# One encoder layer on one core: exponentials kept in PSUM, experts in shifted order with two sums

## Chip, cores, metric

One core of a Trainium2 chip runs the whole layer in one launch. The metric is the device time of one execution, in microseconds (us). TensorE (PE) multiplies, VectorE (DVE), ScalarE (ACT) and GpSimd (POOL) work elementwise, SyncE (SP) issues most transfers. PEld is TensorE's weight load.

## What is computed

```python
# x: (1, 2048, 1024) float32
proj = h @ W_in                       # pool 512 | q latent 256 | kv latent 128 | rope key 32
y_pool = pool_mixer(u_pool)           # windowed means less the channel, linear map per group
s = einsum('bqhd,bkhd->bhqk', q, k) * 96**-0.5     # 8 heads, 64 + 32 channels
y_mla = einsum('bhqk,bkhd->bqhd', softmax(s), v)   # bidirectional, v has 64 channels
h = LN(alpha*h + concat(y_pool, y_mla) @ W_out)
# 64 experts, each token goes to 8 of them with normalised weights
f = sum over its experts e of w_e * (silu(h @ Wg[e]) * (h @ Wu[e])) @ Wd[e]   # 1024 -> 256 -> 1024
f += shared expert of the same shape
out = LN(alpha*h + f)
```

## The kernel before

All products are float32 split in a high part (`fp32r`, what TensorE multiplies in one pass) and a low part (the rest): a product is then high x high + high x low + low x high (`mm3`, `split`).

The stages follow one another: projections and pooling (`project`), attention (`attend`), output projection with the first norm and the routing (`mix_and_route`), the experts with the last norm (`experts`). The attention's main loop and the routed experts' loop run under `manual_schedule`: each engine executes its instructions in the order in which the code issues them. GpSimd's queue also holds the indirect transfers, SP's all plain ones; an instruction that waits holds up everything behind it on its engine.

**Attention.** 8 heads x 4 blocks of 512 queries are 32 blocks; a block takes 8 steps `(n, c)` of 256 keys, each in two halves of 128 keys. A step is issued in this order: `scores` of both halves into one `ps2` tile of two PSUM banks (three products a half); two maxima for a later block, each a product `max_mm` into `psx` and a reduction `max_red`; `exps`, two ACTIVATEs over 1024 columns, one exact (`p`) and one rounded (`ph`), both into SBUF; `low` of the step before, which takes `p - ph` into float16 (`pl`, in steps 2 and 5 half of it on GpSimd) and adds `p` to the row sums on GpSimd; `values` of the step before that, two products of `ph` with 128 columns of values (high and low parts side by side) and two of `pl` with 64 columns of float16 values, one into either half of the same accumulator. Once a block come `max_neg`, `evac` (the two halves of the accumulator are added), `sums` (a product with ones, a reciprocal) and `turn` (transposes; `finish` scales the output). `split_out` splits w_out for the next stage in 16 of the blocks.

**Experts.** `jobs` are three of the shared expert (256 tokens each), 64 routed ones by falling number of tokens, then five more of the shared expert. A routed job has `CAPS[r]` slots: 12 jobs of 376 to 304 and 24 of 296 to 264 slots have three tiles of rows (the third narrow), 28 jobs of 256 have two. In `step(j)`: `load_weights(j+1)` issues three transfers of 1 MB into the three `wst` buffers; `load(j+2)` reads the expert's list of tokens (`idx`) and gathers their rows on GpSimd into the five `xg` buffers; `gate_up(j, 0)`; splits of the next weights; `act`; `columns` (transposes of the next job's rows through `psx`); `gate_up(j, 1)`; more splits; then for each tile `down` and `scatter`, an indirect transfer that adds the tile's rows to `acc` in DRAM. A tile of at most 64 rows goes through `down_narrow`. The rows to be scattered stand in three buffers used in turn (`y_tile`). Two transfers that add to the same tensor are issued one after the other's landing.

**The end.** After the last routed job, `fetch` loads `acc` for all tokens in units of 256; the shared expert's last four jobs add into those units (`add`), the job `late` is added by GpSimd (`first_y`), and `finish(b)` normalises each unit in pieces between the products (`pace`).

Of the kernel before, what the change touches and what calls it, by code (L numbers as in the profile page):

```python
# [52 lines left out]
class Layer:  # L53
    def __init__(self, ctx, tc, io):
# [4 lines left out]
        self.psum = ctx.enter_context(tc.tile_pool(name="psum", bufs=1, space=PSUM))  # L59
        d = self.dram  # L60
        # high and low parts of the heads' operands, channels by tokens
# [8 lines left out]
        self.hx = d.tile([S + 128, HX], FT, name="hx")  # L70
        self.acc = d.tile([S + 128, D], FT, name="acc")
        self.table = d.tile([E * S, 1], I32, name="table")
# [3 lines left out]
    def ps2(self):  # L76
        return self.psum.tile([128, 2, 512], FT, name="ps2", bufs=2)

    def psx(self):
        return self.psum.tile([128, 512], FT, name="psx", bufs=2)  # L80
# [18 lines left out]
    # ------------------------------------------------------------------ projections and pooling  # L99
    def project(self, attention):  # L100
        tc, nc, io = self.tc, self.nc, self.io
        with ExitStack() as ctx, ExitStack() as top:
# [75 lines left out]
            def latents(b):  # L178
                """Tokens on partitions; both norms and the rope of the keys."""
# [32 lines left out]
                # latent channels on partitions  # L212
# [15 lines left out]
            def pool_in(b, g2):  # L228
                """Pooling channels on partitions."""
# [25 lines left out]
            def values(b):  # L255
                qk = QK[b]
                for j in range(4):
# [4 lines left out]
                    # the high part fits float16  # L262
                    v16 = xp.tile([128, H, 64], HF, name="v16", bufs=2)
                    src = ps.rearrange("p (h e) -> p h e", h=H)
                    nc.scalar.activation(v16, src, AF.Copy)
                    nc.scalar.activation(v[:, :, 0:64], v16, AF.Copy)
                    nc.vector.tensor_tensor(v[:, :, 64:128], src, v16, op=OP.subtract)
# [3 lines left out]
            def queries(b):  # L271
# [87 lines left out]
            def weave(main, *sides):  # L359
                """The steps of main with those of the others between them, each from a step on."""  # L360
# [6 lines left out]
            for b in range(NB):  # L367
# [26 lines left out]
                else:  # L394
                    # the attention begins as early as it can
# [37 lines left out]
    def split_out(self, k, half):  # L433
        c = slice(half * 512, (half + 1) * 512)
        self.split(self.woh[k][:, c], self.wol[k][:, c], self.wos[k][:, c])

    def attend(self):
        tc, nc, io = self.tc, self.nc, self.io
        with ExitStack() as ctx:
# [3 lines left out]
            V, V16, Q, NM = {}, {}, {}, {}  # L443
# [22 lines left out]
            def load_values(h):  # L466
                V[h] = kp.tile([128, NT, 128], FR, name="v", bufs=2)
                nc.sync.dma_start(V[h].bitcast(FT), self.vs[:, h].rearrange("(t p) e -> p t e", p=128))
                V16[h] = kp.tile([128, NT, 64], HF, name="v16", bufs=2)

            def cast_values(h):
                nc.scalar.activation(V16[h], V[h][:, :, 0:64].bitcast(FT), AF.Copy)
# [22 lines left out]

            def max_red(h, b, i):
                qt, kb = divmod(i, 4)
                if (h, b) not in NM:
                    NM[h, b] = kp0.tile([128, 4, 4], FT, name="m4", bufs=2)
                nc.vector.reduce_max(NM[h, b][:, qt, kb:kb + 1], MP.pop((h, b, i)), axis=AX.X)  # L500

            # one over the sums of a block's queries, and the maxima of the block after next, queries on partitions
# [25 lines left out]
            def turn(n):  # L528
                """Both as rows: the first on 64 partitions, the maxima on the one that takes them in."""
                rn = rows(n)  # L530
                pt = self.psa()
# [3 lines left out]
                if n >= 0:  # L535
                    finish(n, pt)
                if n + 2 < NBLK:
                    max_row(n + 2, pt[96:97])

            ST, PT, ACC, AV = {}, {}, {}, {}  # L540

            def scores(n, c, half):
                h, b = blocks[n]
                k, q = key_columns(h, (2 * c + half) * 128, 128), Q[h, b]
                if half == 0:
                    ST[n, c] = self.ps2()
                st = ST[n, c]
                nc.tensor.matmul(st[:, half], k[:, 0], q[0:97, 0], start=True, stop=False)
                nc.tensor.matmul(st[:, half], k[0:96, 0], q[0:96, 1], start=False, stop=False)
                nc.tensor.matmul(st[:, half], k[0:96, 1], q[0:96, 0], start=False, stop=True)  # L550

            def exps(n, c):
                st = ST.pop((n, c))
# [1024 lines left out]
```

## Time and profile before

| what | us |
|---|---|
| median of 3 runs | 3168.24 |
| lowest, highest | 3163.23, 3185.31 |
| profiled execution, first to last instruction | 3228.7 |

The profile is of one execution of its own; it gives the span and no other time. Its page says for the whole span that TensorE is busy 90%, VectorE 68%, ScalarE 51%, GpSimd 48%; these are averages over stages with different limits. A busy TensorE is not TensorE at its peak, since its products overlap and their ends are modelled: their starts tell the pace.

### The profile page before, as it was taken

How to read it: one execution, taken by the hardware profiler on the slowest of the kernel's cores; microseconds unless marked ns; L12 is line 12 of the kernel's file. 1: busy time of each engine (PE TensorE's matmuls, PEld its weight loads, DVE VectorE, ACT ScalarE, POOL GpSimd, SP SyncE). 2: the span in 40 equal slices, each digit the busy share in tenths (PEclk: the TensorE clock that was granted, in tenths of full speed). 3: DMA queues.
4: the chain of work that ended last, by engine and by line, in shares of the span. 5: the costliest groups of instructions: out<-in, count | busy, mean ns of one | idle time of the engine just before them, and what ended most of it. 6: DMA issues, size and time to landing. Idle time of an engine off the chain costs nothing. (4 is left out here: it accounts for less than half of the span.)

```text
span 3228.7 us, 44106 instructions
## 1 busy us (share of the span) xinstructions
PE 2896.9 (90%) x16127; PEld 2334.6 (72%) x16127; DVE 2185.6 (68%) x3570; ACT 1661.3 (51%) x2531; POOL 1548.9 (48%) x919
## 2 busy tenths in 40 slices
PE   8998999989989999866799999998998899899986
PEld 6886655555555557645699988787777888888886
DVE  5557999999999996646445555455555555555548
ACT  4444666566656662211255655455555565555554
POOL 2123888788788870455223444444443322223223
PEclk9998999999999999878899999999999999999998
DMA  6555012022111015422578887777777788888873
GB/s 192 211 190 185 19 46 53 28 52 52 47 36 43 20 37 189 144 101 70 177 203 235 251 228 212 208 219 209 221 220 214 222 273 258 249 260 265 275 223 124
DMA packets 175595, 521.43 MB, mean 161 GB/s; under 512 B 37392, under 2 KB 68944, under 8 KB 150032
## 3 DMA queue, kind: packets, MB, share of 16 engines
q1 hardware_dynamic: 130160, 368.44, 33.3%
q0 software_dynamic: 45216, 150.13, 19.6%
q8 instruction: 129, 2.11, 0.3%
q14 instruction: 90, 0.74, 0.1%
HBM read 375.93 MB, written 142.57 MB: 161 GB/s over the span
## 5 line engine op out<-in xcount | busy, mean ns | idle before, releaser
L1510 POOL DMA_INDIRECT acc<-big,idx x164 | 280.3, 1709 | 897.9 <-DMA acc<-big,idx 276.1
L87 DVE TENSOR_TENSOR wl<-wst,wh 128x1024 fp32r<-128x1024 f32 x392 | 470.2, 1225 | 288.1 <-ACT wh L86 277.3
L576 POOL TENSOR_TENSOR acc<-acc,p 128x1024 f32<-128x1024 f32 x186 | 494.6, 2659 | 68.9 <-ACT p L556 63.1
L86 ACT ACTIVATE wh<-wst 128x1024 fp32r<-128x1024 f32 x396 | 403.8, 1053 | 96.1 <-DMA wst<-in_w_up_dram 61.9
L95 PE MATMUL ps<-ht,wh 128*128 128x256 f32 (+10 forms) x1248 | 366.0, 293 | 8.0 <-ACT ht L86 4.1
L96 PE MATMUL ps<-ht,wh 128*128 128x256 f32 (+10 forms) x1248 | 362.6, 291 | 0.0
L97 PE MATMUL ps<-ht,wl 128*128 128x256 f32 (+10 forms) x1248 | 362.3, 290 | 0.0
L500 DVE TENSOR_REDUCE m<-psx 128x1 f32<-128x512 f32 x512 | 339.4, 677 | 23.2 <-PE psx L492 23.0
L556 ACT ACTIVATE p<-ps 128x1024 f32<-128x1024 f32 x256 | 261.8, 1023 | 177.0 <-PE ps L550 120.5
L568 DVE TENSOR_TENSOR pl<-p,ph 128x1024 f16<-128x1024 f32 x192 | 338.2, 1763 | 0.5 <-ACT ph L557 0.5
L95 PE MATMUL ps<-xT,wh 128*128 128x256 f32 (+10 forms) x1056 | 311.0, 295 | 0.0
L96 PE MATMUL ps<-xT,wh 128*128 128x256 f32 (+10 forms) x1056 | 307.8, 291 | 0.0
L97 PE MATMUL ps<-xT,wl 128*128 128x256 f32 (+10 forms) x1056 | 307.6, 291 | 0.0
L557 ACT ACTIVATE ph<-ps 128x1024 fp32r<-128x1024 f32 x256 | 260.7, 1018 | 0.0
L95 PEld LDWEIGHTS ps<-ht,wh 128*128 128x128 f32 x1248 | 238.4, 191 | 12.0 <-ACT ht L86 5.1
L96 PEld LDWEIGHTS ps<-ht,wh 128*128 128x128 f32 x1248 | 238.9, 191 | 2.0 <-DVE ht L87 0.2
L97 PEld LDWEIGHTS ps<-ht,wl 128*128 128x128 f32 x1248 | 239.0, 192 | 0.4
L974 POOL DMA_INDIRECT table<-tok,ri x128 | 131.8, 1030 | 212.4 <-DVE lny L777 119.1
L1421 POOL DMA_INDIRECT xg<-hx,idx x164 | 184.8, 1127 | 88.5 <-issue 30.1
L1146 ACT ACTIVATE big<-psa,wc 128x512 f32<-128x512 f32 (+2 forms) x236 | 160.8, 687 | 104.0 <-DMA acc<-big,idx 46.7
L95 PEld LDWEIGHTS ps<-xT,wh 128*128 128x128 f32 x1056 | 202.9, 192 | 2.9 <-issue 1.6
L1451 PE MATMUL psx<-ident,xg 128*128 128x128 f32 (+6 forms) x1408 | 178.0, 266 | 30.1 <-DMA xg<-hx,idx 25.2
(438 smaller groups left out, 7107.0 us busy)
## 6 DMA issues: line engine op xcount, KB each, us to landing
wst<-in_w_gate_dram SPq DMA_DIRECT2D x64, 1024.0 KB
wst<-in_w_up_dram SPq DMA_DIRECT2D x64, 1024.0 KB
wst<-in_w_down_dram SPq DMA_DIRECT2D x64, 1024.0 KB
xt<-in_x_dram SPq DMA_DIRECT2D x32, 512.0 KB
kn<-stg SPq DMA_DIRECT2D x16, 512.0 KB
vs<-stg SPq DMA_DIRECT2D x16, 512.0 KB
v<-vs SPq DMA_DIRECT2D x8, 1024.0 KB
hx<-r SPq DMA_DIRECT2D x16, 512.0 KB
```

The source lines that it names most:

```text
L86: self.nc.scalar.activation(hi, src, AF.Copy)
L87: (eng or self.nc.vector).tensor_tensor(lo, src, hi.bitcast(FT), op=OP.subtract)
L95: mm(out, lh, rh, start=first, stop=False)
L96: mm(out, lh, rl, start=False, stop=False)
L97: mm(out, ll, rh, start=False, stop=last)
L500: nc.vector.reduce_max(NM[h, b][:, qt, kb:kb + 1], MP.pop((h, b, i)), axis=AX.X)
L556: nc.scalar.activation(p, st, AF.Exp, scale=QK_SCALE)
L557: nc.scalar.activation(ph, st, AF.Exp, scale=QK_SCALE)
L568: nc.vector.tensor_tensor(pl, p, ph.bitcast(FT), op=OP.subtract)
L576: eng.tensor_tensor(a2, ACC[n], p, op=OP.add)
L1421: nc.gpsimd.indirect_dma_start(out=x[0:m], out_offset=None, in_=self.L.hx, in_offset=bass.IndirectOffsetOnAxis(ap=idx[0:m, t:t + 1], axis=0))
L1510: self.nc.gpsimd.indirect_dma_start(out=self.L.acc, out_offset=bass.IndirectOffsetOnAxis(ap=job.idx[0:m, t:t + 1], axis=0), in_=y[0:m], in ...
```

## The change

In the attention PSUM is divided anew (`open_px_attention`): three one-bank tiles `ps` for half steps, one two-bank tile `pxx` for a pair of maxima, one bank `psm` for sums and turned rows, and the two banks `psa`. `exps` works by halves: it writes the rounded exponentials to SBUF and the exact ones over the scores in PSUM. `low` subtracts from PSUM on VectorE, a half at a time, the first half in the same step, the second in the next. The row sums are taken of the rounded part (`add`, on GpSimd); the low part's sum comes from a column of ones beside the values, so the low product has 65 columns, in `fp32r`, into an accumulator of its own. `values_low` stands between the halves of the scores, in the third step of a block (`c == 2`) behind them; `evac_low`, `evac_high` stand first there. Two maxima are one pair, with one reduction over 1024 columns. ScalarE's copies for `evac`, `sums` are put off to the start of the next step (`rest`). `split_out` subtracts on GpSimd. The sum `acc2` is filled with zeros in 16 transfers during the attention.

For the routed experts `step_routed` takes the place of `step`: `find(j+3)` reads the list one job earlier and ahead of the weights, `down` of a job runs behind the next job's `gate_up(.., 0)`, its tiles in turn with `columns`. Second tiles are scattered into `acc2`. A tile of up to 64 rows goes through one `psx` bank. At the end `fetch` adds `acc2` by a second, accumulating transfer on GpSimd's queue, and the job after `late` is put into a buffer and added later (`second_y`, `sum_up`). Splits of the shared expert's weights at the end of the routing go to VectorE.

```diff
+            def scores(n, c, half):
+                st = ST[n, c, half] = self.pxp.tile([128, 512], FT, name="ps", bufs=3)
...
+            def exps(n, c, half):
+                    PT[n, c] = wk.tile([128, 2, 512], FR, name="ph", bufs=5), wk.tile([128, 2, 512], FR, name="pl", bufs=4)
+                nc.scalar.activation(ph[:, half], st, AF.Exp, scale=QK_SCALE)
+                nc.scalar.activation(st, st, AF.Exp, scale=QK_SCALE)
...
+            def low(n, c, half):
+                ph, pl = PT[n, c]
+                nc.vector.tensor_tensor(pl[:, half], ST.pop((n, c, half)), ph[:, half].bitcast(FT), op=OP.subtract)
+            def values_low(n, c):
+                    nc.tensor.matmul(AV[n][1][0:65], VV[blocks[n][0] % 2][:, t, 64:129], pl[:, half],
+                                     start=(t == 0), stop=(t == NT - 1))
...
+            def evac_low(n):
+                nc.vector.tensor_tensor(o, AV[n][1][0:65], bot, op=OP.add)
+                eng.tensor_tensor(ACC[n][64:65], ACC[n][64:65], o[64:65], op=OP.add)
+            def evac_high(n):
+                nc.vector.tensor_tensor(o[0:64], hi[0:64], o[0:64], op=OP.add)
...
                 if live:
                     scores(n, c, 0)
+                for f in rest:
+                    f()
+                if n and c == 2:
+                    evac_low(n - 1)
+                    evac_high(n - 1)
+                for m in mx:
+                    max_pair(*m)
+                if live:
+                    exps(n, c, 0)
+                if c != 2:
+                    for v in vs:
+                        values_low(*v)
                 if live:
                     scores(n, c, 1)
+                    exps(n, c, 1)
+                    add(n, c)
+                if c == 2:
+                    for v in vs:
+                        values_low(*v)
                 if s and (s - 1) // 8 < NBLK:
+                    low(*divmod(s - 1, 8), 1)
+                for m in mx[-1:]:
+                    max_pair_red(*m)
+                if live:
+                    low(n, c, 0)
+                for v in vs:
+                    values_high(*v)
+                if n and c == 1:
+                    rest.append(lambda hi=AV[n - 1][0]: nc.scalar.activation(bot[0:64], hi[64:128], AF.Copy))
+                if c == 4 and 1 <= n <= NT:
+                    nc.sync.dma_start(self.acc2[(n - 1) * 128:n * 128].rearrange("p (q d) -> p q d", q=2),
+                                      z[:, None, :].to_broadcast([128, 2, 512]))
...
+            def step_routed(j):
+                job, nxt = jobs[j], jobs[j + 1]
+                find(j + 3)
+                load_weights(j + 1)
+                load(j + 2)
+                ex.weights_of(nxt)
+                self.gate_up(job, 0)
+                before = behind.pop() if behind else []
+                for t in range(max(len(before), len(nxt.rows))):
+                    if t < len(before):
+                        before[t]()
+                    if t < len(nxt.rows):
+                        ex.columns(nxt, t)
+                for u in ("g", 0), ("u", 0):
+                    self.split_unit(nxt, u)
+                ex.act(job, 0)
+                self.gate_up(job, 1)
+                for u in ("g", 1), ("u", 1):
+                    self.split_unit(nxt, u)
+                ex.act(job, 1)
+                for u in ("d", 0), ("d", 1):
+                    self.split_unit(nxt, u)
+                behind.append([lambda t=t, m=m: down(j, t, m) for t, m in enumerate(job.rows)])
...
     def scatter(self, job, t, y, m):
-            out=self.L.acc, out_offset=bass.IndirectOffsetOnAxis(ap=job.idx[0:m, t:t + 1], axis=0),
+            out=self.L.acc2 if t == 1 else self.L.acc,
...
             def fetch(b):
-                nc.sync.dma_start(A[b], self.acc[b * 256:(b + 1) * 256].rearrange("(t p) d -> p t d", p=128))
+                nc.sync.dma_start(A[b], self.acc[r].rearrange("(t p) d -> p t d", p=128))
+                nc.gpsimd.dma_start(A[b], self.acc2[r].rearrange("(t p) d -> p t d", p=128), accum_op=OP.add)
...
-            for b in LATE[:2] + EARLY:
+            for b in LATE[:3] + EARLY:
                 fetch(b)
```

## Rows read from the trace of the kernel before

**Rows 1.** Windows: stretch, length; PE, PEld, DVE, ACT, POOL busy; clock, DMA share, GB/s

```profile
300.00:1220.00 920.00, 845.63 (x3442) 532.35 (x3443) 888.17 (x915) 557.47 (x631) 746.91 (x315) 0.97 0.17 43
...
1600.00:3116.00 1516.00, 1410.05 (x9450) 1267.34 (x9448) 840.50 (x1429) 833.72 (x1420) 549.17 (x355) 0.98 0.79 232
3116.00:3229.00 113.00, 82.48 (x528) 74.25 (x528) 80.70 (x194) 49.13 (x83) 41.49 (x18) 0.86 0.46 177
```

**Rows 2.** Line 556: count, ns shortest/median/longest, first and last start in us

```profile
L556 ACT ACTIVATE p<-ps x256: 1003/1024/1031, 300.4 to 1213.2; 128x1024 f32<-128x1024 f32 x128
```

**Rows 3.** Groups on VectorE, 330 to 1190 us: busy us, mean ns | idle before, releaser

```profile
L568 DVE TENSOR_TENSOR pl<-p,ph 128x1024 f16<-128x1024 f32 x179 | 316.9, 1771 | 0.0
L500 DVE TENSOR_REDUCE m<-psx 128x1 f32<-128x512 f32 x474 | 314.1, 676 | 18.0 <-PE psx L492 18.0
L565 DVE TENSOR_TENSOR pl<-p,ph 128x512 f16<-128x512 f32 x60 | 169.2, 2820 | 0.0
...
L610 DVE TENSOR_TENSOR o<-psa,bot 64x512 f32<-64x512 f32 x30 | 20.5, 683 | 5.8 <-ACT bot L608 5.8
```

**Rows 4.** Timeline of TensorE, one attention step: start us, duration us, what

```profile
709.74 0.50 PE L548 MATMUL ps<-q,kk 97*128 97x512 f32 x1
710.07 0.40 PE L549 MATMUL ps<-q,kk 96*128 96x512 f32 x1
710.31 0.40 PE L550 MATMUL ps<-q,kk 96*128 96x512 f32 x1
...
711.70 0.63 PE L590 MATMUL psa<-ph,v 128*128 128x512 f32 x2
712.26 0.41 PE L592 MATMUL psa<-pl,v 128*64 128x512 f16 x2
712.60 0.50 PE L548 MATMUL ps<-q,kk 97*128 97x512 f32 x1
```

**Rows 5.** Windows cut at experts: two of 256 slots, five of 256, four of 312, four of 280

```profile
2566.00:2603.00 37.00, 37.00 (x273) 34.61 (x272) 23.50 (x37) 23.87 (x36) 11.70 (x8) 1.00 0.88 263
2703.70:2807.50 103.80, 94.26 (x682) 85.86 (x680) 58.82 (x91) 58.97 (x90) 30.45 (x20) 1.00 0.81 257
1759.90:1854.60 94.70, 94.70 (x610) 87.03 (x610) 56.47 (x104) 56.57 (x105) 43.62 (x28) 1.00 0.86 245
2111.10:2214.20 103.10, 93.80 (x609) 81.75 (x608) 56.40 (x104) 54.64 (x105) 45.07 (x27) 0.97 0.74 211
```

**Rows 6.** Timeline of GpSimd and ScalarE, an expert of 280 slots

```profile
2124.02 1.58 POOL L1510 DMA_INDIRECT acc<-big,idx  x1 [10.08 <-issue]
...
2134.88 1.26 ACT L1146 ACTIVATE big<-psa,wc 128x512 f32<-128x512 f32 x2 [4.56 <-DMA acc<-big,idx]
2135.54 1.40 POOL L1510 DMA_INDIRECT acc<-big,idx  x1 [7.03 <-DMA acc<-big,idx]
...
2137.25 1.98 POOL L1421 DMA_INDIRECT xg<-hx,idx  x1 [0.30 <-PE psa L1502]
```

**Rows 7.** Groups on TensorE once a block, 330 to 1190 us: sums and turned rows

```profile
L599 PE MATMUL psa<-ones,af 128*128 128x2 f32 x240 | 31.6, 254 | 0.0
L534 PE MATMUL psa<-ident,rn 128*97 128x128 f32 x120 | 21.3, 302 | 1.9 <-DVE rn L514 1.9
```

**Rows 8.** Timeline of ScalarE: two copies of 512 columns out of PSUM, merged

```profile
2119.03 1.07 ACT L86 ACTIVATE xT<-psx 128x512 fp32r<-128x512 f32 x2
```

**Rows 9.** Lines 576 and 580: GpSimd's row sums, ns shortest/median/longest

```profile
L576 POOL TENSOR_TENSOR acc<-acc,p x186: 2353/2694/3367, 311.3 to 1193.2; 128x1024 f32<-128x1024 f32 x186
...
L580 POOL TENSOR_TENSOR af<-acc x31: 2133/2144/2162, 331.5 to 1196.4; 128x512 f32<-128x512 f32 x31
```

**Rows 10.** Windows of the end

```profile
3130.00:3140.00 10.00, 5.86 (x27) 5.35 (x26) 5.43 (x19) 8.52 (x16) 2.47 (x2) 0.66 1.03 420
...
3160.00:3170.00 10.00, 7.42 (x44) 7.19 (x45) 9.90 (x15) 5.77 (x9) 6.07 (x3) 0.66 0.39 157
```

**Rows 11.** Timeline of GpSimd: the first addition after the fetches

```profile
3127.79 4.68 POOL L1321 TENSOR_TENSOR wst<-wst,big 128x1024 f32<-128x1024 f32 x2 [19.84 <-DMA wst<-acc]
```

More of the change, by code (lines that the diff above doesn't have):

```diff
@@ L71, in __init__ @@
         self.acc = d.tile([S + 128, D], FT, name="acc")
+        self.acc2 = d.tile([S + 128, D], FT, name="acc2")
         self.table = d.tile([E * S, 1], I32, name="table")
@@ L466, in load_values @@
             def load_values(h):
[L467 to L472, printed above, removed]
+                if VV[h % 2] is None:
+                    v = VV[h % 2] = kp.tile([128, NT, 132], FR, name=f"v{h % 2}")
+                    nc.gpsimd.tensor_copy(v[:, :, 128:129], ones[:, 0:NT, None])
+                nc.sync.dma_start(VV[h % 2][:, :, 0:128].bitcast(FT), self.vs[:, h].rearrange("(t p) e -> p t e", p=128))
             def load_q(h, b):
@@ L571, in low @@
                 else:
-                    if c == 1:
-                        a2 = wk.tile([128, 2, 512], FT, name="acc")
-                    else:
-                        a2 = ACC[n]
+                    a2 = wk.tile([128, 2, 512], FT, name="acc") if c == 1 else ACC[n]
                     eng.tensor_tensor(a2, ACC[n], p, op=OP.add)
@@ L655, in attend @@
                         load_keys(n // NB + 1)
-                        load_values(n // NB + 1)
                     if n + 2 < NBLK:
                         load_q(*blocks[n + 2])
-                mx = list(map(max_items, range(done, min(done + 3, LEAD + 2 * s + 2, 16 * NBLK))))
+                if c == 2 and n % NB == 0 and n // NB + 1 < H:
+                    load_values(n // NB + 1)
+                mx = [blocks[i // 8] + (i % 8,) for i in range(done, min(done + 2, LEAD + s, 8 * NBLK))]
@@ L660, in attend @@
                 done += len(mx)
+                vs = [divmod(s - 2, 8)] if s >= 2 and (s - 2) // 8 < NBLK else []
                 if live:
                     scores(n, c, 0)
-                for m in mx[0:1]:
-                    max_mm(*m)
+                for f in rest:
+                    f()
+                rest = []
+                if n and c == 2:
[3 more added lines that the diff above has]
+                    max_pair(*m)
+                    if m is not mx[-1]:
+                        max_pair_red(*m)
@@ L725, in fill_tables @@
         nc.gpsimd.memset(z, 0.0)
-        for dst, n in ((self.hx, HX), (self.acc, D)):
+        for dst, n in ((self.hx, HX), (self.acc, D), (self.acc2, D)):
             for c in range(0, n, 512):
@@ L1172, in down @@
                 a = A.get(job.shared)
-                if j > late:
+                if j == late + 1:
+                    second_y.append(ex.down(job, t, m, copy, job.xs[t][:, 0:D]))
+                elif j > late:
                     ex.down(job, t, m, add(job.shared, t), a[:, t])
@@ L1183, in down @@
                 else:
-                    spare = t == 1 and all(len(jobs[i].rows) == 2 for i in (j, j + 1))
-                    ex.scatter(job, t, ex.down(job, t, m, weigh(job, t), spare=spare), m)
+                    ex.scatter(job, t, ex.down(job, t, m, weigh(job, t)), m)
             work = []
@@ L1255, in experts @@
                 for j in range(4, late + 1):
-                    if j == late:
-                        more = nc.values_load(self.ovi[0:1, 2, 0:1], min_val=0, max_val=128)
+                    if j < late:
+                        step_routed(j)
+                        continue
+                    more = nc.values_load(self.ovi[0:1, 2, 0:1], min_val=0, max_val=128)
+                    behind[:] = [lambda before=behind.pop(): [f() for f in before]]
                     step(j)
```

225 lines of the change are left out of this document (116 added, 109 removed).

## Prediction

> **What bounds the kernel now.** I read the stages first [rows 1]: busy time of each engine in the three stretches that the change touches. The attention takes 920 us of the 3228.7 us span, with VectorE busy for 888 of them (97%) and TensorE for 846. The experts take 1516 us, with TensorE busy for 1410 and the DMA engines for 79%. The end, after the last routed expert, takes 113 us. The profiled span is 60 us above the median of the runs, 3168.24 us; it is the only time that this execution gives. I make the sum against the span and scale the result by 3168.24 / 3228.7 = 0.9813.
>
> Attention: 256 steps of 128 x 1024 scores begin over 912.8 us, so 3.58 us a step, 28.6 us a block of eight [rows 2]. VectorE's groups say what fills them [rows 3]: a low part of 1024 columns takes 1771 ns, of 512 in the two steps of a block where GpSimd takes the other half 2820 ns; each of the two maxima of a step 676 ns. The same engine in the same stage adds 512 columns in 683 ns when one operand lies in PSUM, with GpSimd busy for 747 of the 920 us. Two operands in SBUF are what costs here. TensorE's order in time [rows 4] shows the next limit: a 512-column product starts 0.23 us after the one before it, but the step as a whole takes at least 2.86 us (709.74 to 712.60) where nothing waits.
>
> Experts: four stretches cut where a first product begins [rows 5]. In them an expert issues 136 matmuls with two tiles and 152 with three. Four experts of 312 slots take 94.7 us (23.7 each, TensorE never idle); four of 280 take 103.1 (25.8 each); five of 256 take 103.8 (20.8); but two of 256 right after a long stop took 37.0 (18.5), TensorE never idle. So the later experts lose some 2 to 4 us each. Where to: GpSimd's own time line [rows 6]. A scatter-add into `acc` issued at 2124.02 lets the next one go only at 2135.54, and the gather for a later expert stands behind it until 2137.25. On ScalarE a weighted copy out of PSUM waits 4.56 us for the same landing, because its row buffer is still being read; TensorE stands still then. Every scatter waits for the one before it, two or three an expert, so a chain of landings sets the pace.
>
> **The change part by part: attention.** VectorE per block after: 16 low halves with one operand in PSUM at 683 ns, 10.9 us; eight maxima over 1024 columns; three more half tiles per block (two evacuations, the product) 2.0; two small ones 0.3. No row shows a maximum over 1024: at least 0.68, at most twice 676 ns = 1.35; I take 1.27, near the upper end. Sum 10.9 + 10.2 + 2.3 = 23.4 us, against 28.6 now.
>
> TensorE per block after: twelve 512-column products a step at 0.233, 22.4 us; the sums and the turned rows stay, busy 31.6 and 21.3 us over 30 blocks [rows 7], at most 1.8 a block. That is 24.2, more than VectorE: the bound moves to TensorE. The low products are no more float16 on half of the columns, two side by side; they become two full products of 65 columns. In the rows the pair takes 0.34 us (712.26 to 712.60), the two high products ahead of it 0.56 instead of 0.46, and the first score after it 0.33 instead of 0.24; changing form costs 0.1 us twice a step. New: 0.46 + 0.46 with no change of form, 0.1 to 0.2 us less a step.
>
> The Trainium skill, TensorEngine Tiling (Array Packing), Overview, says that a stationary side of at most 64 columns may run two at once, which speaks against this edit: by that alone the step would grow by 0.23 us, 59 us in all, and the result would be 3006. The same page, Key Properties, says that changing the tiling mode drains the engine; the trace agrees with both, 0.34 us for the pair and 0.1 us at either change [rows 4], so that the changes eat what the pair gains.
>
> The third step, walked in queue order with these prices and a step of 2.8. `evac_low` and `evac_high` stand first on VectorE there, behind a copy on ScalarE that itself waits for the second half of the step before (0.7 us in). Copy 0.7 to 1.3, evacuations to 2.0 and 2.7, then the low half to 3.3 (1.9 late), the maxima to 4.6, the next low half to 5.3. `values_low`, moved behind both scores (1.9 us in), waits for 2.0, and `values_high` for 2.7: 0.4 lost. In the step after, the maxima's products come at 4.0 and find their tile taken until 4.6: 0.6 to 0.7 lost. Then VectorE has caught up. 1.1 us a block; nothing if the copy comes early, twice that if VectorE stays behind. So 24.2 + 1.1 = 25.3, rounded to 25.2 since 1.8 is an upper bound: 32 x 28.6 - 32 x 25.2 = 108 us gained.
>
> ScalarE: four exponentials of 512 at half of 1.07 us [rows 8], 32 x 0.535 = 17.1 a block, and 1.6 for the rest: hidden. No row shows ScalarE writing to PSUM. Cheaper changes nothing, for it is not the bound; at twice the price for the 16 in place it would need 27.3 and cost 67 us. I take the price of a copy into SBUF, the nearest row.
>
> GpSimd: seven additions at 2.69 and one at 2.14 [rows 9], one row of 512 and in 16 blocks a split of w_out, each at most 2.14: 21.0 to 25.2, hidden. The additions' own shortest is 2.35, so there is room once VectorE reads PSUM. The 16 zero fills of `acc2` (0.5 MB each) and the values' load, moved to step 2 on SP's queue, lie where the DMA engines are 17% busy [rows 1]: nothing; uncovered, each fill would cost 1.2 us at 420 GB/s [rows 10]. Casts gone from ScalarE: nothing. Closing and opening the PSUM pools twice makes the first users wait for the last readers: 0 to 7 us, I take 4 lost. In the projections one ScalarE copy a tile of values goes: 0 to 8 us, I take 3 gained. The splits moved from GpSimd to VectorE at the end of the routing: plus or minus 5, I take nothing.
>
> **Experts.** `acc2` takes the second tile of each expert: two-tile experts then chain one landing an expert per sum, three-tile ones two. At 11.5 us from issue to issue [rows 6], one landing fits into 18.5 us and two just into 22 (the first and third tile's issues lie a tile apart already); the chain falls behind TensorE. `find` reads the list a step earlier and stands ahead of the weights on SP's queue, so a gather waits for no list. Running `down` behind the next expert's first product hides the hidden layer's split. What TensorE then needs: two tiles 18.5, the pair in the row; three tiles of 280 what those of 312 took less 32 columns in 96 products, 96 x 0.23 x 32 / 512 = 1.4, so 23.7 - 1.4 = 22.3. What is late next is the weights: they have three buffers, and the DMA share is 0.88 at 18.5 us an expert [rows 5]. I add 0.3 and 0.4 for that: 18.8 and 22.7. By the table of capacities there are 28 experts of 256 (two at 18.5, the others taken at 20.8, mean 20.6), 24 of 264 to 296 (taken at 25.8) and 12 larger ones, for which I take 0.5: 28 x 1.8 + 24 x 3.1 + 12 x 0.5 = 130 us gained. Bounds: 150 at 18.5 and 22.0, 50 if the transfers take over.
>
> **The end.** `fetch` gets a second, accumulating transfer on GpSimd's queue, six of them ahead of the two additions of `first_y`; each must wait for its first megabyte. Now the first addition starts at 3127.8, after 19.84 us of waiting [rows 11]; six fetches instead of five at 420 GB/s are 2.5 us more, the accumulate itself 2.5 (as plain loads) to 7 (as the scatter waits in [rows 6]), and the last scatter comes some 6 us later in TensorE's order, since a first product (48 of an expert's 136 matmuls) now runs ahead of it. VectorE is 99% busy in the middle of this stage [rows 10], so a late start moves the end: 2 to 25 us, I take 12 lost.
>
> Sum: -108 - 130 + 12 + 4 - 3 = -225 us; 3228.7 - 225 = 3004; x 0.9813 = 2948. I say 2950.
>
> **The rivals.** *Transfers take over (0.20).* The chain goes, but 0.88 of the DMA engines at 18.5 us leaves little, and the scatters land late because they share the engines with 3 MB of weights. For it: the share is 0.81 even at 20.8 us [rows 5]. Against it: the two experts at 18.5, and 420 GB/s in the last stage [rows 10]. Experts at 20.0 and 24.6 gain 28 x 0.6 + 24 x 1.2 + 6 = 52: 3082, 3024 scaled. The Trainium skill, DMA: Bandwidth & Descriptors, Rules for kernel authors, says that transfers issued from SP and GpSimd run on the same 16 engines, so a second sum adds no bandwidth; the trace agrees in so far as share and rate rise together [rows 5].
>
> *ScalarE bounds the attention (0.12).* In-place exponentials at twice the price, 27.3 us a block: gain 41 instead of 108, 3071, 3013 scaled.
>
> *The change doesn't do what it says (0.06).* The gathers stay late for another reason (five row buffers for two experts of three tiles), so that only the hidden split is gained, 64 x 0.5 = 32, and the third step's stall doubles, 108 - 35 = 73: 73 + 32 - 13 = 92, 3078 scaled. For it: the gathers' idle time ends with the scatter ahead of them in the rows, which hides what else they wait for.
>
> *Slower (0.04).* Three half-score buffers replace two whole ones. With a turnaround T from the first score to the end of the low part, a step can't be shorter than 2T/3. My walk gives T = 3.3 us; if T passes 6.06 us the attention loses the 117 us that the rest gains, at 6.5 it gives 4.33 us a step: +193 - 117 = +76, 3243 scaled. For it: both exponentials and a maximum of 1.27 stand in each turn; against it: no row near doubles.
>
> **How the numbers follow.** The forecast has 0.58 of the chance, and its own range is 2890 to 3010. The range reaches to the transfers' and ScalarE's cases and, below, to experts at 150 with no stall in the third step: 2870 to 3040. A difference under 1% (32 us) is no difference here: the runs lie 0.7% apart. Faster 0.93; same 0.03 (half of the third rival, should both of its parts fail); slower 0.04, the last rival.
>
> **What would show it.** Attention: step near 3.1 us, low halves near 0.68, maxima near 1.27, VectorE below 95%, TensorE waiting in steps 2 and 3 of a block alone. Experts: no wait of a scatter for a landing, 18.8 and 22.7 us an expert, DMA share near 0.88. End: first addition some 10 us later against the last matmul of the routed experts. Wrong if ScalarE writes PSUM slowly, if the share sticks at 0.8 with TensorE waiting for weights, or if the accumulating fetches hold up the last norms.

## The result, and the profile after

| | kernel before | changed kernel |
|---|---|---|
| median of four runs, us | 3165.73 | 3027.15 |
| lowest, highest | 3154.89, 3185.31 | 3020.71, 3041.38 |
| profiled execution, first to last instruction | 3228.7 | 3019.8 |

The ratio is 0.9556, with a 95% interval of 0.9502 to 0.961: 4.4% faster. The forecast was 2950 us, in a range of 2870 to 3040. The executions of the kernel before spread from 3129 to 3252 us over this study and the one profiled first, at 3228.7, was one of the long ones, while those of the changed kernel lie between 3018 and 3041.

The stages of the changed kernel, in windows cut where the first exponential, the first product of the first routed expert, of the first one of 296 and of 256 slots, and of the job `late` begin (busy us and count of PE, PEld, DVE, ACT, POOL; clock, DMA share, GB/s); they answer to [rows 1, 5, 10]:

```profile
301.90:1113.00 811.10, 782.28 (x3421) 583.18 (x3420) 675.72 (x915) 603.85 (x1133) 633.37 (x306) 0.99 0.24 59
1113.00:1497.90 384.90, 295.26 (x1474) 243.24 (x1473) 214.45 (x716) 91.56 (x146) 140.09 (x135) 0.88 0.40 138
1497.90:1796.80 298.90, 292.07 (x1809) 265.51 (x1808) 159.60 (x276) 162.92 (x271) 110.88 (x76) 0.99 0.79 223
1796.80:2341.30 544.50, 538.23 (x3643) 478.23 (x3642) 334.48 (x596) 327.60 (x586) 250.45 (x166) 1.00 0.81 244
2341.30:2852.20 510.90, 510.64 (x3819) 479.08 (x3817) 326.40 (x505) 331.49 (x510) 166.59 (x111) 1.00 0.98 292
2852.20:3019.80 167.60, 107.13 (x690) 95.55 (x688) 89.48 (x202) 65.81 (x113) 55.04 (x28) 0.84 0.64 182
```

Attention: 811 us for 32 blocks, with VectorE busy for 83% of it (97% in [rows 1]) and TensorE for 96%. The 28 experts of 256 slots: TensorE busy 510.64 of 510.90, so 18.2 us each, at a DMA share of 0.98. Its two costliest groups on VectorE, 330 to 1090 us, against [rows 3]:

```profile
L584 DVE TENSOR_TENSOR pl<-ps,ph 128x512 fp32r<-128x512 f32 x483 | 326.7, 681 | 51.4 <-ACT ps L565 51.4
L613 DVE TENSOR_REDUCE m<-pxx 128x2 f32<-128x1024 f32 x238 | 288.9, 1214 | 29.3 <-PE pxx L608 29.3
```

The lines of the exponentials (count, ns shortest/median/longest, first and last start), against [rows 2, 8]:

```profile
L564 ACT ACTIVATE ph<-ps x512: 583/598/604, 301.9 to 1113.0; 128x512 fp32r<-128x512 f32 x171
...
L565 ACT ACTIVATE ps<-ps x512: 587/592/606, 302.4 to 1113.5; 128x512 f32<-128x512 f32 x171
```

The low half costs 681 ns, a pair of maxima 1214, an exponential into SBUF 598 and one over its own scores in PSUM 592. TensorE's order in time, one step from its first score to that of the next (start us, duration us), against [rows 4]:

```profile
711.56 0.40 PE L555 MATMUL ps<-q,big 97*128 97x512 f32 x1
...
712.26 0.61 PE L608 MATMUL pxx<-big,q 96*128 96x512 f32 x2
712.71 0.63 PE L593 MATMUL psa<-pl,v 128*65 128x512 f32 x2
...
713.88 0.63 PE L600 MATMUL psa<-ph,v 128*128 128x512 f32 x2
714.35 0.40 PE L555 MATMUL ps<-q,big 97*128 97x512 f32 x1
```

Twelve products in 2.79 us, 0.2325 each, with none that waits. GpSimd among the two-tile experts, against [rows 6]:

```profile
2498.62 1.60 POOL L1611 DMA_INDIRECT acc<-big,idx  x1 [9.41 <-ACT big L1206]
2502.31 1.58 POOL L1611 DMA_INDIRECT acc<-big,idx  x1 [2.08 <-ACT big L1206]
2504.19 1.89 POOL L1520 DMA_INDIRECT xg<-hx,idx  x1 [0.30 <-DVE xT L99]
...
2516.77 1.61 POOL L1611 DMA_INDIRECT acc<-big,idx  x1 [9.40 <-ACT big L1206]
```

No scatter waits for a landing; what they wait for is their data, every 18.15 us. At the end, GpSimd's first addition, against [rows 11]:

```profile
2902.22 2.33 POOL L1420 TENSOR_TENSOR wst<-wst,big 128x1024 f32<-128x1024 f32 x1 [9.72 <-DMA wst<-acc]
```

TensorE's longest waits there (us, times, longest):

```profile
PE psa L1587 <- DVE xT L1223: 8.2, 2, 7.1
PE psx L1551 <- DMA xg<-hx: 6.3, 1, 6.3
PE psa L1587 <- ACT xg L1215: 5.9, 1, 5.9
```

Pieces of the chain that ended last (start us, us, what):

```profile
2884.15 34.87 DMA xg<-hx
...
2967.27 9.08 DMA xT<-acc
...
2976.88 8.59 DMA xT<-acc
```

The rows of the shared expert's job after next wait 35 us behind the fetches, and the last unit comes in two transfers, one after the other, 9.1 and 8.6 us. From the last routed product to the end it takes 156.6 us (2863.2 to 3019.8), before 133.3 (3095.4 to 3228.7): 23 us more. The first addition starts 38.9 us after that product, before 32.4.

### The profile page after: what moved, and what is told of

The parts are those of the page before. It is cut to its first block, busy times and chain, and to the rows that moved or that the text cites. A ratio compares the mean times of both kernels' runs of the same rounds, so it can differ in the third digit from the quotient of the medians.

```text
span 3019.8 us, 44329 instructions
## 1 busy us (share of the span) xinstructions
PE 2797.8 (93%) x16127; PEld 2369.0 (78%) x16127; DVE 1971.4 (65%) x3555; ACT 1705.9 (56%) x2995; POOL 1422.3 (47%) x915
## 5 line engine op out<-in xcount | busy, mean ns | idle before, releaser
L99 DVE TENSOR_TENSOR wl<-wst,wh 128x1024 fp32r<-128x1024 f32 x396 | 481.4, 1255 | 94.5 <-ACT wh L98 90.4
L575 POOL TENSOR_TENSOR acc<-acc,ph 128x1024 f32<-128x1024 f32 x190 | 455.7, 2398 | 103.6 <-ACT ph L564 101.0
L1611 POOL DMA_INDIRECT acc<-big,idx x164 | 257.7, 1572 | 424.5 <-ACT big L1206 393.9
L564 ACT ACTIVATE ph<-ps 128x512 fp32r<-128x512 f32 x512 | 305.6, 597 | 204.0 <-PE ps L557 192.3
L584 DVE TENSOR_TENSOR pl<-ps,ph 128x512 fp32r<-128x512 f32 x512 | 346.2, 682 | 58.3 <-ACT ps L565 58.3
L1206 ACT ACTIVATE big<-psa,wc 128x512 f32<-128x512 f32 (+2 forms) x264 | 181.6, 688 | 276.4 <-issue 140.2
L613 DVE TENSOR_REDUCE m<-pxx 128x2 f32<-128x1024 f32 x248 | 301.1, 1214 | 35.7 <-PE pxx L608 35.7
L565 ACT ACTIVATE ps<-ps 128x512 f32<-128x512 f32 x512 | 303.7, 593 | 0.0
L99 DVE TENSOR_TENSOR ht<-psx,ht 128x512 fp32r<-128x512 f32 (+4 forms) x200 | 126.0, 662 | 218.0 <-ACT ht L98 205.3
L99 DVE TENSOR_TENSOR xT<-psx,xT 128x512 fp32r<-128x512 f32 (+5 forms) x184 | 114.6, 657 | 177.2 <-ACT xT L98 177.1
```

Source lines behind the costliest of these rows:

```text
L99: (eng or self.nc.vector).tensor_tensor(lo, src, hi.bitcast(FT), op=OP.subtract)
L564: nc.scalar.activation(ph[:, half], st, AF.Exp, scale=QK_SCALE)
L565: nc.scalar.activation(st, st, AF.Exp, scale=QK_SCALE)
L575: eng.tensor_tensor(a2, ACC[n], p, op=OP.add)
L584: nc.vector.tensor_tensor(pl[:, half], ST.pop((n, c, half)), ph[:, half].bitcast(FT), op=OP.subtract)
L613: nc.vector.reduce_max(maxima(h, b)[:, qt, 2 * kp:2 * kp + 2], MP.pop((h, b, i)), axis=AX.X)
```

## The experiments

**The kernel before, again.** 

> The kernel before, unchanged, profiled a second time. Its first profile spans 3228.7 us, its four timed runs have a median of 3165.7. Theory: the first profile caught a slow execution, and a new one spans 3150 to 3190, with the missing 40 to 75 us in one stage that can be named; I expect them in the experts, since the attention's steps repeat evenly. Rival: the profiler itself stretches this kernel, and the new span is again near 3229, all stages alike.

It spans 3138.9 us. Its windows, cut as above:

```profile
304.80:1220.00 915.20, 836.35 (x3413) 524.59 (x3412) 882.66 (x908) 554.61 (x628) 749.51 (x315) 0.97 0.17 43
1220.00:1609.90 389.90, 297.57 (x1476) 244.27 (x1475) 216.12 (x710) 92.49 (x146) 148.57 (x139) 0.89 0.40 136
1609.90:1904.40 294.50, 293.53 (x1842) 269.80 (x1841) 164.48 (x290) 168.03 (x290) 112.41 (x76) 1.00 0.82 234
1904.40:2437.80 533.40, 533.26 (x3642) 481.14 (x3641) 334.03 (x621) 330.26 (x611) 245.87 (x167) 1.00 0.86 249
2437.80:3006.90 569.10, 529.07 (x3810) 483.17 (x3809) 329.95 (x502) 330.49 (x504) 161.02 (x109) 1.00 0.84 259
3006.90:3138.90 132.00, 100.95 (x665) 91.14 (x663) 86.11 (x204) 56.73 (x97) 44.56 (x20) 0.89 0.48 164
```

In the first profile the same stages take 912.8, 393.3, 294.5, 617.2, 577.4 and 133.1 us. One stage makes most of the difference, 84 of 90 us: the 24 experts of 296 to 264 slots, 533 instead of 617 us. In the first profile, cut 3 us wider, it shows so:

```profile
1900.00:2520.00 620.00, 563.84 (x3662) 492.15 (x3661) 337.41 (x621) 328.02 (x613) 266.66 (x166) 0.97 0.75 214
```

TensorE stands idle there for 56 us, and with nearly the same products it is busy for some 28 us longer, at a granted clock of 0.97 instead of 1.00. In the second profile 280 slots take 22.3 us each with TensorE never idle, where [rows 5] have 25.8. GpSimd's time line shows the difference:

```profile
2107.66 1.64 POOL L1510 DMA_INDIRECT acc<-big,idx  x1 [2.32 <-ACT big L1146]
2114.80 1.60 POOL L1510 DMA_INDIRECT acc<-big,idx  x1 [5.50 <-issue]
...
2122.00 1.42 POOL L1510 DMA_INDIRECT acc<-big,idx  x1 [2.69 <-DMA acc<-big,idx]
```

Three scatters follow each other at 7.2 us, not 11.5 as in [rows 6]: three fit into 22.3. So the chain of landings has a short and a long rhythm with the same instructions, and most of what the forecast let the 24 experts gain is there only in executions with the long one. What sets off the long one is not shown.

**Either half of the change alone.** 

> The change's attention and projections with the experts, their loop and the end of the kernel before (one sum, no zero fills). Theory: the stages add up, the attention takes 811 us as in the changed kernel (25.4 us a block), and the time is 105 us under the kernel before, 3060. Rival: a faster attention hands the later stages a worse state (the clock, or the first transfers of the experts), so that less than 80 us arrive, 3090 or more.

> The attention of the kernel before with the change's experts, second sum, zero fills and end. Theory: what the whole change gains beyond the attention's 105 is what the experts give, about 35 us by the timed runs, so 3130; three-tile experts at 22.7 us, two-tile ones at 18.15 as in the changed kernel. Rival: the experts give what the two traces show, 91 us with the longer end, 3075, and the attention gives less than its trace shows.

```diff
 att_only: class Experts, experts(), beyond() of the kernel before; no acc2
 exp_only: project(), attend() of the kernel before; acc2 and its zero fills added
```

Attention alone: 3102.2 us, ratio 0.9758 (0.9628 to 0.9888); its attention takes 809.4 us, as in the changed kernel. That half of the theory holds. The time misses 3060 and falls where the rival has it, at 3090 or more. In the profiled execution the 24 experts ran in the long rhythm (601 us, 68 more than in the second profile of the kernel before), which is more than what is missing there; the other three runs have no profile, so whether a shorter attention brings that rhythm on stays open. Experts alone: 3132.9 us, ratio 0.9882 (0.9784 to 0.998), with the theory's 3130; 544.4 us for the 24, 510.7 for the 28, and 916.5 for its attention. The two ratios multiply to 0.964, and the whole has 0.9556 and, in its second series below, 0.9601: the parts add up within what the spread of the kernel before lets one see.

**What the chain waits for.** 

> The changed kernel with every scatter into one sum and no accumulating transfers at the end (the zero fills stay). Theory: the chain of landings is back: 2 x 11.5 us for a two-tile expert where TensorE needs 18.15, so 20.5 or more each, three-tile ones 25; experts lose 28 x 2.4 + 24 x 2.3 = 120, the end gains 20, together 3127. Rival: the shifted order and the early lists are what freed the experts; then the second sum is only a cost at the end, and the time is near 3007.

> The kernel before with the second sum alone: second tiles go to it, it is filled with zeros during the attention, and every fetch at the end gets its accumulating transfer. Order of the experts, lists and attention stay. Theory: two chains of landings are enough, so the later three-tile experts take 533 us as in the undisturbed execution and never more, the 28 two-tile ones 28 x 18.4 = 515, the end 20 more: 3139 - 54 + 20 = 3105, with runs close to each other. Rival: the shifted order and the early lists are needed as well, since a gather still waits behind the scatters; two-tile experts stay at 19.5 or more, 546 in all, and the time is 3130 or more.

> The kernel before, its routed experts' weights cut to an eighth of their bytes (the experts compute with a repeated part of each matrix); everything else as it was. Theory: a scatter lands in 7 us by itself and in 11 to 12 with weights beside it, so that without them the gap between scatters that wait for each other is 7.0 to 7.3 throughout: two-tile experts at 18.4 us, 515 in all instead of 570 to 577, the later three-tile ones at 533, 3085 in all. Rival: the chain costs 10 to 12 us by itself, by its own rows and their number; the gaps stay and the two-tile experts stay at 20.5.

```diff
 one_sum (from the changed kernel)
-            out=self.L.acc2 if t == 1 else self.L.acc,
+            out=self.L.acc,
-                nc.gpsimd.dma_start(A[b], self.acc2[r]..., accum_op=OP.add)
 two_old (from the kernel before)
+            out=self.L.acc2 if t == 1 else self.L.acc, ...
+                nc.gpsimd.dma_start(A[b], self.acc2[r]..., accum_op=OP.add)
 light_w (from the kernel before)
-            nc.sync.dma_start(s, src.rearrange("o p (k f) -> p (o k) f", k=8))
+                nc.sync.dma_start(s[:, 0:1], v[:, 0:1])
...
```

Without the second sum the changed kernel takes 3078.4 us (0.9692, 0.9594 to 0.979), some 50 more than with it; the theory has 3127, the rival 3007. The 24 experts need 591.8 us and the 28 need 556.9, in the shifted order and with early lists:

```profile
1807.60:2399.40 591.80, 559.19 (x3642) 490.84 (x3641) 348.17 (x599) 325.13 (x587) 260.53 (x165) 0.96 0.80 224
2399.40:2956.30 556.90, 524.94 (x3818) 488.31 (x3816) 325.21 (x502) 327.13 (x507) 174.02 (x111) 0.99 0.90 268
```

That the shifted order and the early lists free the experts by themselves is refuted. With the second sum alone the kernel before takes 3131.9, its runs between 3126.6 and 3140.9. Its 24 and 28 experts:

```profile
1923.40:2456.80 533.40, 533.26 (x3642) 481.15 (x3641) 348.66 (x620) 329.98 (x611) 270.97 (x167) 1.00 0.85 249
2456.80:2971.40 514.60, 514.60 (x3810) 486.89 (x3809) 330.06 (x502) 331.84 (x505) 147.53 (x110) 1.00 0.91 288
```

TensorE never waits: the second sum does all of it. The time lies above the theory's 3105, where the rival has it (3130 or more), though the two-tile experts are at 18.4 us and not at the rival's 19.5: the end grew by 36 us (132.0 to 167.7), not 20, and the attention and the routing of the profiled execution took 11 and 7 us more than in the second profile of the kernel before. With an eighth of the weights' bytes (the experts compute with a repeated part of each matrix) and one sum both stages take the same 533.4 and 514.6 us; the whole takes 3098.9, where the theory has 3085. In the 28 experts a scatter of 128 rows then takes 6.0 us from its issue to its last packet by the median, and 8.5 in the second profile of the kernel before. So it is the weights beside it that make a landing late, and not their own arrival that TensorE waits for: with all of the weights and two sums the stages are as short. GpSimd's waits of scatters for landings (us, times, longest), in the second profile of the kernel before and with light weights:

```profile
POOL acc L1510 <- DMA acc<-big,idx: 117.2, 17, 12.1
```

```profile
POOL acc L1520 <- DMA acc<-big,idx: 120.1, 22, 5.7
```

The longest is halved. The sum of the waits is not, as GpSimd has time to wait; by the lengths of the stages, what decides is whether two landings fit into an expert.

**Where the exact exponentials stand.** 

> The changed kernel with the exact exponentials written to SBUF, three buffers of half a step, as the kernel before did; nothing else moves. Theory: the PSUM operand is what made the low part cheap. A half from two SBUF operands takes 886 ns or more (half of 1771), up to 2820 beside GpSimd; VectorE then needs at least 14.2 + 10.2 + 2.3 = 26.7 us a block and bounds the attention again, 855 us or more instead of 811, up to 1000. Rival: the new order of the step did it and TensorE is the bound; VectorE has 15% to spare, and the attention stays at 811 to 825 us.

```diff
-                nc.scalar.activation(st, st, AF.Exp, scale=QK_SCALE)
+                p = ST[n, c, half] = wk.tile([128, 512], FT, name="p", bufs=3)
+                nc.scalar.activation(p, st, AF.Exp, scale=QK_SCALE)
```

The attention takes 1051 us, 240 more than changed and 136 more than in the second profile of the kernel before, at a granted clock of 0.91 instead of 0.99 and 0.97, and the whole 3284.3. The theory holds in its effect, and is wrong in its price. The line of the low halves:

```profile
L585 DVE TENSOR_TENSOR pl<-p,ph x512: 670/680/2897, 308.8 to 1359.6; 128x512 fp32r<-128x512 f32 x171
```

Two instructions that overlap, in the timelines of VectorE and of GpSimd:

```profile
704.96 2.50 DVE L585 TENSOR_TENSOR pl<-p,ph 128x512 fp32r<-128x512 f32 x1
```

```profile
704.52 2.38 POOL L576 TENSOR_TENSOR acc<-acc,ph 128x1024 f32<-128x1024 f32 x1 [1.17 <-ACT ph L564]
```

Two operands in SBUF cost 680 ns as well, by the median. But 229 of the 512 take over 1 us, 2.13 on the mean, and each of the 200 that take more than 1.5 began while a GpSimd instruction was at work and ends 0.55 us after the GpSimd instruction beside it has ended (704.52 + 2.38 = 706.90, and 704.96 + 2.50 = 707.46): it stands still until GpSimd is done. In the changed kernel the low halves, with one operand in PSUM, take 668 to 694 ns, although GpSimd was at work when some 370 of the 512 began. The Trainium skill, SBUF — State Buffer, section "SBUF: two separate sides", says so: an instruction of VectorE with two SBUF inputs and one of GpSimd that reads SBUF exclude each other, and whichever starts first keeps the other out for all of its length. The trace agrees for the 200 that GpSimd was ahead of.

**The third step.** 

> The changed kernel with the low value products of the third step in their ordinary place, between the halves of the scores. Theory, by the walk of the prediction: they come 0.8 us before the evacuation of the accumulator is done, TensorE stands still, and the wait is on the path: 31 x 0.8 = 25 us, attention 836 us, the third step from 3.25 to 4.0 us. Rival: TensorE only waits there instead of in the steps behind it, where VectorE is late anyway; attention 811 us within 5.

```diff
-                if c != 2:
-                    for v in vs:
-                        values_low(*v)
+                for v in vs:
+                    values_low(*v)
...
-                if c == 2:
-                    for v in vs:
-                        values_low(*v)
```

TensorE's wait for the evacuation (us, times, longest) between 350 and 1050 us, here and in the changed kernel:

```profile
PE psa L593 <- DVE o L631: 26.3, 28, 1.0
```

```profile
PE psa L593 <- DVE o L631: 6.7, 28, 0.3
```

The wait of 0.9 us a block is there, as the theory has it, but the attention takes 813.3 us against 811.1 and 813.2 in two profiles of the changed kernel, a block 25.09 against 25.08: the third step grows from 3.25 to 3.45 us and the fourth shrinks from 3.51 to 3.31. The rival holds: to put `values_low` behind both scores in the third step is worth nothing here.

**The changed kernel again, another end, another order.** 

> The changed kernel, unchanged, for a second profile and more times. Theory: with two sums no scatter waits for a landing on the path, so its three-tile experts cannot fall into the slow rhythm: the span lies within 25 us of the first (3019.8), the later three-tile experts take 544 us again, and the runs lie within 1% of each other while those of the kernel before spread over 2 to 3%. Rival: the changed kernel has a slow rhythm too that its first profile missed; then a run or this profile lies 50 us or more higher.

> The changed kernel with the end reordered: rows of the shared expert's job after next are loaded ahead of the fetches; the units into which TensorE's products are added are all fetched at once, with one of the others, and the two remaining units later, into buffers that are done early. Theory: the end is long because two units are fetched late, each behind an output and as two transfers one after the other (9.1 and 8.6 us), and because the rows stand behind 12 MB; then 6 us of TensorE's wait for rows and 15 of the 27 us after its last product go: 3005 against 3027. Rival: the end is bound by VectorE's and GpSimd's norms or by the accumulating transfers as such; then the time stays within 8 us of the changed kernel's.

> The changed kernel with the order of the kernel before for the experts of three tiles, and the shifted order for those of two; two sums and the end as changed. Theory: with two sums the old order needs 22.28 us for 280 slots where the shifted one takes 22.7, and 294.5 instead of 299 for the twelve largest: 533 + 294 instead of 544 + 299, so 15 us less than the changed kernel. Rival: the difference was an accident of the executions (this stage's end is cut at another place); the sum of both stages stays at 843 and the time with it.

```diff
 tail_order (from the changed kernel)
...
-            for b in LATE[:3] + EARLY:
-                fetch(b)
+            load(late + 3, 1)
+            for b in (LATE[0], EARLY[0]):
+                fetch(b)
+            load(late + 3)
+            for b in LATE[1:]:
+                fetch(b)
...
 hybrid (from the changed kernel)
-                    if j < late:
+                    if j < late and len(jobs[j].rows) == 2:
                         step_routed(j)
                         continue
+                    if j < late:
+                        step(j)
+                        continue
```

The changed kernel: 3025.5 us, six runs between 3017.6 and 3036.5 beside runs of the kernel before between 3129 and 3227; 544.7 and 510.9 us for the 24 and the 28. No run and neither profile shows a long rhythm.

The reordered end: 3032.9, no gain, against the theory and within the 8 us of its rival. TensorE's wait for rows is gone, and in its place TensorE waits 12.4 us for a copy on ScalarE, which stands behind the first sums of a norm, which wait for GpSimd's first addition.

The mixed order: 3010.4 us (3006.1 to 3014.4), 15 less than the changed kernel on the same chip, as expected. Its three stages:

```profile
1503.10:1799.10 296.00, 293.56 (x1842) 269.77 (x1841) 169.05 (x281) 167.32 (x281) 119.50 (x78) 1.00 0.85 234
1799.10:2332.50 533.40, 533.26 (x3642) 481.14 (x3641) 347.07 (x597) 328.64 (x588) 268.98 (x167) 1.00 0.85 249
2332.50:2836.90 504.40, 503.42 (x3786) 473.36 (x3785) 321.64 (x497) 324.02 (x498) 164.56 (x109) 1.00 0.98 291
```

The 24 experts go back from 544.7 to 533.4. That the 28 show 504 instead of 511 us lies in the cut: the three `down` of the last three-tile expert now stand ahead of it, in the stage of the 24. So the sum is what counts: the three stages take 1333.8 us, 20 less than in the two profiles of the changed kernel (1354.3 and 1353.9), and this is what the shifted order costs there with three tiles. It is the fastest of all, 0.955 of the kernel before (0.9479 to 0.962).

> The kernel of the run before (old order for experts of three tiles, shifted for two) with one more edit at the end: the first unit is fetched ahead of the others and alone, behind half of the rows of the shared expert's job after next, and both of its additions on GpSimd stand ahead of the other units' accumulating transfers. Theory: ScalarE stands 12 us behind these additions, and TensorE behind ScalarE, since the first unit's two transfers share the DMA engines with five others (9 and 13 us where 1 MB alone takes 2.5 to 5); now the first addition comes 9 us or more earlier, the wait for rows (6 us) goes, and the time is 2998 against 3010. Rival: what bounds the end is the sum of the transfers and norms, so that each wait moved comes back later, as with the reordered end: 3008 to 3015.

```diff
 first_alone (from the mixed order)
+            with tc.manual_schedule():
+                load(late + 3, 1)
+                fetch(LATE[0])
+                for t, y in enumerate(first_y):
+                    a = A[LATE[0]][:, t]
+                    nc.gpsimd.tensor_tensor(a, a, y, op=OP.add)
+                load(late + 3)
+                for b in LATE[1:3] + EARLY:
+                    fetch(b)
...
```

3019.5 us (3014.4 to 3029.3), not 2998; this is another chip, and of the kernel before it is 0.9547, as the mixed order is 0.955. The first fetch, alone, takes 10.1 us until its accumulating transfer can be issued (2882.38 to 2892.45), and that one another 14.2 until the addition starts at 2906.66, 41 us after the last routed product, where the mixed order has 38.5. So the other fetches are not what makes the first plain transfer long, and the first addition does not come earlier. Of the accumulating transfer the run does not tell: SyncE issued the five other plain fetches between 2890.0 and 2894.8, around its issue, so it did not have the DMA engines to itself. The theory's forecast falls; its cause is untested in that half. Both additions are done 45.7 us after the last routed product, where the mixed order has 55.5. The end takes 161.4 us against 167.4, but the routing of the profiled execution took 401 against 385 us with the same instructions, at a granted clock of 0.86 against 0.88, so whether this end is a gain stays open.

## Why the prediction was right, and where it was off

The sign and the range held, and of the mechanisms the two that carry the gain: an operand in PSUM frees VectorE, and a second sum frees the experts from the chain of landings. The shifted order, which the forecast counted in, costs the three-tile experts some 20 us, by the mixed order. The point was 77 us low, and one step carries most of that: **"x 0.9813"**, the scaling of the sum by the ratio of the runs' median to the profiled span. The sum itself forecast a span of 3004 us, and the changed kernel's is 3019.8, 16 more. The scaling treats the 60 us by which the profile lay above the runs as spread over everything. By the two profiles they lay in the experts of three tiles, in a rhythm that no profile of a kernel with the second sum shows: the changed kernel had no surplus left to scale away. That took off 55 us without cause.

Term by term, in spans against the first profile:

- Attention, -108: it is -102 (912.8 to 811.1). A block takes 25.4 us by the mean, 25.1 by the median; the forecast was 25.2. The low half was put at 683 ns and takes 681, the pair of maxima at 1.27 us and takes 1.21, TensorE's products at 0.233 and take 0.2325. TensorE's waits between 350 and 1050 us come to 16.9 in 28 blocks, 0.6 each where the walk had 1.1. By the estimate that the prediction drew from the Trainium skill, TensorEngine Tiling (Array Packing), Overview, the step would grow by 0.23 us. Where nothing waits it shrank, from 2.86 to 2.79. The reason given for VectorE, "two operands in SBUF are what costs", names the right operand and half of the cause: the price was paid for meeting GpSimd, as the kernel with the exponentials in SBUF shows.
- Experts, -130: from the first routed product to the last it is -124 (1488.9 to 1365.4), but only -31 against the second profile of the kernel before (1396.7), and with the end, which grew by 24 against that profile, 7 us remain. That -130 came out is luck in so far as the profile at hand was one with the long rhythm; against an execution with the short one nearly all of the change's gain is the attention's. The experts of 280 slots were forecast at 22.7 us and take 22.7, those of 256 at 18.8 and take 18.2. What was wrong was to take as fixed the 25.8 with which the first was compared, and the 11.5 us from scatter to scatter [rows 6], taken as the price of a landing: it is 7.2 in the short rhythm.
- The end, +12 with bounds of 2 to 25: +23. The mechanism is the one named. With one sum in the same order the end takes 144.8 us instead of 167.6, so the accumulating transfers cost 23. They were priced nearer to plain loads (2.5) than to the scatters' waits (7); the last unit's takes 8.6, behind a plain one of 9.1. The first addition was forecast some 10 us later against the last routed product and comes 6.5 later.
- Pools and projections, +1: the stage ahead of the attention went from 300.4 to 301.9 us, the routing from 393 to 385. In the profiles of this study the routing takes 377 to 410 us at granted clocks of 0.85 to 0.89, whichever kernel runs, so nothing can be read from it.

Of the rivals, "transfers take over" gave 3024 and would have been closest, for a wrong reason: the share did rise to 0.98, and TensorE does not wait. ScalarE is not the bound (74% busy). The ring of three buffers costs at most the 51 us that VectorE waits for exponentials, on an engine that is busy for 83% and not the bound.

## What to carry to other kernels

When a profiled execution lies above the runs, find the stage that holds the surplus, by a second profile where there is one, before any of its durations becomes a price; a ratio over the whole span is no correction. Where transfers add to one place in a chain, ask how many landings fit into the period, with loads beside them and without: near the edge the time jumps, and a second destination that is summed later is worth what it costs at the end. And before an elementwise instruction is called dear, look at its shortest duration: a long mean over a short minimum is a wait.

## What was not expected of the hardware

- A subtraction of 128 x 512 on VectorE with two SBUF operands that meets a GpSimd instruction already at work ends 0.55 us after it; with one operand in PSUM it takes its 0.68 us whether GpSimd is at work or not. GpSimd gains too: its addition of 512 columns takes 1291 ns in the changed kernel, 2144 in [rows 9].
- From issue to its last packet, a scatter of 128 rows in the 24 experts takes 5.9 us by the median in the second profile of the kernel before and 8.4 (up to 11.7) in the first, with the same instructions.
- Writing exponentials over their own scores in PSUM costs ScalarE no more than writing them to SBUF, 592 against 598 ns for 128 x 512.
- A DMA share of 0.98 goes with a TensorE that is busy for 510.6 of 510.9 us, so the share alone does not say that transfers bound a stage.
